# Rotating the first keys and queries on VectorE, with finer filling, in a fused attention and RWKV kernel

## The chip, the cores and the metric

One core of one Trainium2 chip runs the whole program. The metric is the device time of one execution in microseconds (us), the median of several runs. The profile is that of one execution, and its times count from the first instruction.

## The reference, cut to what matters

The program is a first block of two layers and a second block of one layer on 512 tokens of width 1024, all in float32. The diff touches the first block:

```python
def first_block(x, p, ...):
    for i in range(2):
        h = rms_norm(x, norm_g[i])
        y = mixer_a(...) if i == 0 else mixer_b(h, b_w_in, b_q_norm, b_k_norm, b_w_out)
        x = x + y                                   # the mixer ends with @ w_out
        g = sigmoid(rms_norm(x, ple_norm_g[i]) @ ple_w_gate[i])
        x = x + g * (p[i] @ ple_w_proj[i])
    return rms_norm(x, final_norm_g)

def mixer_b(h, ...):                                # 16 query heads, 4 key heads of width 64
    q, k, v, gate = split(h @ w_in)
    q = rope(rms_norm(q, q_norm_g)); k = rope(rms_norm(k, k_norm_g))
    o = softmax(q k^T / 8) v                        # all 512 keys
    return (o * silu(gate)) @ w_out
```

`rope` multiplies each row by a table of cosines and adds the row with swapped quarters times a table of sines. The kernel folds the norm's gain (and 1/8 for the queries) into the tables.

## The kernel before

The program is written in Python over tiles. A planner puts each engine's instructions in an order by a model of their times, with the order of the program as the priority; each engine then runs its own list strictly in that order, and waits are by tile and buffer.

Matrix products keep float32 precision by splitting each operand into a high part (rounded) and a low part (the rest) and adding three products. So each weight unit (512 KB) is loaded by SP's DMA queue (`wraw`), copied to its high part by ScalarE (`whi`, line 147) and subtracted to its low part (`wlo`, line 148) by the engine that `self.lo` names: VectorE, or GpSimd once `mixer_b` has made its first queries.

`rows` makes token-major products (line 200), `cols` feature-major ones (lines 183 to 185). Results lie in PSUM banks by tag: two banks each of `mm`, `sc`, `tr` and `u`.

`mixer_b` first makes keys and values, then the queries of group 0 (four heads), then loops over four groups. `qk_rows` makes 256 tokens' worth of keys or queries in each of two passes: products into a bank; square on ScalarE into `b_scr` (line 529); sum, reciprocal root and multiply on VectorE into `b_qn` (lines 531 to 535); rotation on GpSimd, one multiply by the cosines into `b_rot` (line 540) and four by the sines into a second `b_scr` (line 546); an add on VectorE (line 550). `b_scr` and `b_qn` have one buffer each. Then follow two steps that transpose the result (line 555) and split it into `b_Q` (or `b_Kh` and `b_Kl`); the second half of each step in `group` makes a gate by `cols`.

In the loop a group has four sets of two blocks (`b_block`); a block makes the scores of 128 queries for two heads (lines 638 and 639), their negated maximum `b_mn` on VectorE (641), the exponential into `b_P` on ScalarE (644; six buffers), the reciprocal `b_rd` (646), the scaling on GpSimd (647), transposes (654), a split into `b_ph` and `b_pl` (216 and 217) and the products with V (661). After each set, `next(fill)` runs one of the four steps of the next group's `group` generator, so that TensorE has other work; in the last group the steps are parts of the output projection over the first six of eight feature blocks (`first`), at most six of eight parts.

After the mixer the rest of `first` is run; then `load_p` loads p on SP's queue (line 391) and splits it into `p_hi` and `p_lo`. In layer 0, `rope_tables` also loads the tables (lines 505 to 510), and `products` multiplies them by the gains on VectorE (line 515, 16 instructions). Then come the last part of the output projection, with its add to x on VectorE (line 342), the norm, and the gate with p's projection (`ple`).

Of the kernel before, what the change touches and what calls it, by code (L numbers as in the profile page):

```python
# [10 lines left out]
F32 = mybir.dt.float32  # L11
# [8 lines left out]
KT = 8  # L20
TT = 4
# [102 lines left out]
class Net:  # L124
# [50 lines left out]
    def cols(self, key, act):  # L175

        nc = self.nc
        self.fetch(key)
        wh, wl = self.w.pop(key)
        ah, al = act  # L180
        ps = self.bank("mm")
        for kt in range(KT):
            nc.tensor.matmul(ps, lhsT=wh[:, kt], rhs=ah[:, kt], start=kt == 0, stop=False)  # L183
            nc.tensor.matmul(ps, lhsT=wh[:, kt], rhs=al[:, kt], start=False, stop=False)  # L184
            nc.tensor.matmul(ps, lhsT=wl[:, kt], rhs=ah[:, kt], start=False, stop=kt == KT - 1)  # L185
        return ps
# [201 lines left out]
    def load_p(self, l, pool):  # L388
        nc = self.nc
        raw = pool.tile([P, 2, S], F32, name="p_raw", bufs=1)  # L390
        nc.sync.dma_start(out=raw, in_=self.a["pT"][l])
        hi = pool.tile([P, 2, S], F32R, name="p_hi", bufs=1)
        lo = pool.tile([P, 2, S], F32R, name="p_lo", bufs=1)
        self.split(hi, lo, raw)
        return hi, lo
# [102 lines left out]
    def rope_tables(self, keep, pool, name, scale):  # L498
# [13 lines left out]
        def products():  # L512
            for j, o in enumerate((c, s)):
                for tt in range(TT):
                    nc.vector.scalar_tensor_tensor(o[:, tt], t[:, j, tt], scale, g[:, j], op0=OP.mult, op1=OP.mult)
# [3 lines left out]
    def qk_rows(self, pool, us, act, tabs, evac, bank="mm"):  # L519

        nc = self.nc
        c, s = tabs
        rot = pool.tile([P, TT, 256], F32, name="b_rot", bufs=1)
        for tp in range(2):
# [3 lines left out]
            sq = pool.tile([P, 512], F32, name="b_scr", bufs=1)  # L528
# [5 lines left out]
            qn = pool.tile([P, 512], F32, name="b_qn", bufs=1)  # L534
# [5 lines left out]
            nc.gpsimd.tensor_tensor(r4, q4, c[:, ts, None, :].to_broadcast([P, 2, 4, HD]), op=OP.mult)  # L540
            t2 = pool.tile([P, 512], F32, name="b_scr", bufs=1)
            for tt in range(2):
                for hf in range(2):
                    vw = lambda ap: ap.rearrange("p (h s f e) -> p h s f e", h=4, s=2, f=2)
                    sv = s[:, 2 * tp + tt].rearrange("p (s f e) -> p s f e", s=2, f=2)[:, :, hf]
                    nc.gpsimd.tensor_tensor(vw(t2[:, 256 * tt:256 * tt + 256])[:, :, :, hf],
# [4 lines left out]
            yield  # L551
        for pr in range(2):
            ps = self.bank("tr")
            for t in range(TT):
                nc.tensor.transpose(ps[:, t * P:(t + 1) * P], rot[:, t, pr * P:(pr + 1) * P], self.ident)
            evac(pr, ps)
            yield

    def mixer_b(self, act, oT, pool, last):
# [17 lines left out]
        for tp, _ in enumerate(self.qk_rows(pool, us, act, tk, put_k, "u")):  # L577
# [7 lines left out]
        def group(g, Q, gates):  # L585

            gp = g % 2
            self.fetch(("b_q", g, 0), ("b_q", g, 1))
# [9 lines left out]
            for n, _ in enumerate(self.qk_rows(pool, us, act, tq, put_q, "sc" if g == 0 else "mm")):  # L598
                if n > 1:
                    ps = self.cols(("b_g", 2 * g + n - 2), act)  # L600
# [9 lines left out]
        self.lo = nc.gpsimd  # L610
        for g in range(4):
            Qn, gn = [], []
            fill = group(g + 1, Qn, gn) if g < 3 else last
            for pr in range(2):
                i = 2 * g + pr
                for bp in range(2):
                    U = self.bank("u").rearrange("p (b e q) -> p b e q", b=2, e=2)
                    for bb in range(2):
                        self.b_block(pool, Q[2 * pr:2 * pr + 2], Kh[:, g], Kl[g // 2][:, g % 2], V[:, :, g], 2 * bp + bb, U[:, bb])
# [8 lines left out]
                    for _ in range(1 if g < 3 else 2 - bp):  # L628
                        next(fill, None)
# [774 lines left out]
def tile_net(ctx: ExitStack, tc: tile.TileContext, a, out, stop=None):  # L1404
# [22 lines left out]
    with ExitStack() as blk:  # L1427
# [25 lines left out]
        for l in range(2):  # L1453
            oT = N.new_act()
            with open_pool("pm%d" % l) as pool:
                first = N.out_proj(l, oT, (0, 1, 2))
                if l == 0:
                    N.mixer_a(act, oT, pool)
                else:
                    N.mixer_b(act, oT, pool, (next(first, None) for _ in range(6)))  # L1460
                for _ in first:
                    pass
# [3 lines left out]
            with open_pool("pn%d" % l) as pool:  # L1466
                act = N.new_act()
                pT = N.load_p(l, pool)
                g = N.gain(pool, "ple_norm_g", l)
                if l == 0:  # L1470
# [246 lines left out]
```

## Time and profile before

| | |
|---|---|
| median of 3 runs | 1243.92 us (1239.63 to 1244.29) |
| the profiled execution | 1243.45 us, span 1241.4 us |
| mean granted TensorE clock | 0.960 of 2.4 GHz |
| TensorE busy | 1145.3 us (92%) |
| VectorE, ScalarE, GpSimd busy | 849.4 us (68%), 624.0 us (50%), 425.6 us (34%) |

The span is from the first to the last instruction. Layer 0's last part of the output projection runs from about 287 us, the second mixer from about 380 to 647 us. A busy share is a mean over stages with different limits, so the rows that matter are those of single stretches.

### The profile page before, as it was taken

How to read it: one execution, taken by the hardware profiler on the slowest of the kernel's cores; microseconds unless marked ns; L12 is line 12 of the kernel's file. 1: busy time of each engine (PE TensorE's matmuls, PEld its weight loads, DVE VectorE, ACT ScalarE, POOL GpSimd, SP SyncE). 2: the span in 40 equal slices, each digit the busy share in tenths (PEclk: the TensorE clock that was granted, in tenths of full speed). 3: DMA queues.
4: the chain of work that ended last, by engine and by line, in shares of the span. 5: the costliest groups of instructions: out<-in, count | busy, mean ns of one | idle time of the engine just before them, and what ended most of it. 6: DMA issues, size and time to landing. Idle time of an engine off the chain costs nothing.

```text
span 1241.4 us, 20546 instructions
## 1 busy us (share of the span) xinstructions
PE 1145.3 (92%) x7176; PEld 1006.2 (81%) x7176; DVE 849.4 (68%) x2089; ACT 624.0 (50%) x1355; POOL 425.6 (34%) x571
## 2 busy tenths in 40 slices
PE   7999999997999879999999989798899789899995
PEld 6898989885889767888877889688898678798884
DVE  6566666655677678887766663488786924688846
ACT  5565565533552438676655642433544223267842
POOL 0021211110112555857320011163444623357851
PEclk9999999998999979999999999889789989899998
DMA  6333333213133210102132345684667543712511
GB/s 244 115 107 99 107 94 103 88 52 123 51 123 98 68 51 18 40 30 68 52 112 84 104 142 190 209 269 146 197 186 183 172 136 102 235 48 71 194 35 68
DMA packets 87041, 143.25 MB, mean 115 GB/s; under 512 B 21525, under 2 KB 52245, under 8 KB 86938
## 3 DMA queue, kind: packets, MB, share of 16 engines
q1 hardware_dynamic: 72632, 134.53, 34.5%
q10 hardware_dynamic: 13730, 5.31, 1.7%
q0 software_dynamic: 576, 2.10, 0.5%
q8 instruction: 56, 0.92, 0.3%
q14 instruction: 47, 0.39, 0.1%
HBM read 114.12 MB, written 27.79 MB: 114 GB/s over the span
## 4 chain that ended last, share of the span: by engine, by line
PE 64%; DVE 18%; DMA 8%; ACT 4%; issue 3%; POOL 1%; SPq 1%; ACTq 0%; DVEq 0%; POOLq 0%
PE mm L200 23%; PE mm L183 5%; PE mm L184 5%; PE mm L185 5%; PE mm L211 3%; PE u L661 2%; PE sc L200 2%; PE tr L654 2%; DVE KT L951 2%; PE tr L487 1%; PE ch L987 1%; DVE big L953 1%; PE u L1357 1%; PE tr L313 1%; DVE wlo L148 1%
## 5 line engine op out<-in xcount | busy, mean ns | idle before, releaser
L200 PE MATMUL mm<-whi,act 128*128 128x256 f32 (+2 forms) x1344 | 359.7, 325 | 16.5 <-DVE x L342 7.6
L200 PE MATMUL mm<-wlo,act 128*128 128x256 f32 (+2 forms) x896 | 288.6, 322 | 0.0
L200 PEld LDWEIGHTS mm<-whi,act 128*128 128x128 f32 x1344 | 241.7, 195 | 38.5 <-DVE x L342 10.5
L200 PEld LDWEIGHTS mm<-wlo,act 128*128 128x128 f32 x896 | 175.4, 196 | 10.1 <-issue 0.2
L147 ACT CAST whi<-wraw 128x1024 fp32r<-128x1024 f32 (+1 forms) x128 | 133.2, 1043 | 94.4 <-PE mm L200 36.1
L200 PE MATMUL mm<-whi,half 128*128 128x256 f32 (+1 forms) x448 | 146.0, 328 | 3.0 <-DVE half L217 3.0
L148 DVE TENSOR_TENSOR wlo<-wraw,whi 128x1024 fp32r<-128x1024 f32 x83 | 107.3, 1297 | 48.7 <-ACT whi L147 47.0
L148 POOL TENSOR_TENSOR wlo<-wraw,whi 128x1024 fp32r<-128x1024 f32 (+2 forms) x45 | 106.9, 2377 | 75.7 <-ACT whi L147 58.4
L183 PE MATMUL mm<-act,whi 128*128 128x512 f32 x312 | 125.8, 403 | 2.6 <-DVE b_qn L535 2.6
L185 PE MATMUL mm<-act,wlo 128*128 128x512 f32 x312 | 124.5, 399 | 0.0
L200 PEld LDWEIGHTS mm<-whi,half 128*128 128x128 f32 x448 | 88.4, 198 | 9.8 <-DVE half L217 4.0
L479 POOL TENSOR_SCALAR a_P<-a_P,a_rd 128x256 f32<-128x256 f32 x64 | 33.0, 519 | 156.5 <-DVE a_rd L478 143.8
L184 PE MATMUL mm<-half,whi 128*128 128x512 f32 x200 | 79.1, 396 | 0.0
L183 PEld LDWEIGHTS mm<-act,whi 128*128 128x128 f32 x312 | 60.1, 192 | 14.5 <-issue 3.5
L185 PEld LDWEIGHTS mm<-act,wlo 128*128 128x128 f32 x312 | 59.8, 192 | 11.8
L647 POOL TENSOR_SCALAR b_P<-b_P,b_rd 128x512 f32<-128x512 f32 x64 | 45.9, 724 | 44.5 <-DVE b_rd L646 32.9
L644 ACT ACTIVATE b_P<-sc,b_mn 128x512 f32<-128x512 f32 x64 | 44.1, 690 | 23.7 <-DVE b_mn L641 21.2
L217 DVE TENSOR_TENSOR b_pl<-tr,b_ph 128x512 fp32r<-128x512 f32 x64 | 43.7, 683 | 16.0 <-ACT b_ph L216 15.7
L473 DVE CUSTOM_DVE_ANT_0 a_P<-sc,a_bias 128x256 f32<-128x256 f32 x64 | 26.1, 422 | 34.7 <-PE tr L487 20.1
L641 DVE TENSOR_REDUCE b_mn<-sc 128x1 f32<-128x512 f32 x64 | 43.6, 684 | 8.1 <-PE sc L639 7.4
L385 POOL TENSOR_TENSOR x<-pu,x 128x512 f32<-128x512 f32 x8 | 10.3, 1293 | 111.6 <-DVE pu L383 111.6
L1343 POOL TENSOR_SCALAR n_P<-n_P,b_rd,n_gl 128x128 f32<-128x128 f32 (+3 forms) x64 | 39.3, 624 | 25.6 <-DVE b_rd L1341 6.2
(385 smaller groups left out, 2899.2 us busy)
## 6 DMA issues: line engine op xcount, KB each, us to landing
wraw<-in_wstream SPq DMA_DIRECT2D x133, 512.0 KB, 3.7
a_bias<-in_bias SPq DMA_DIRECT2D x16, 384.0 KB, 3.1
rkv<-d_raw SPq DMA_DIRECT2D x16, 384.0 KB, 4.9
d_raw<-act SPq DMA_DIRECT2D x8, 384.0 KB, 6.0
xf<-x SPq DMA_DIRECT2D x4, 512.0 KB, 3.7
d_low<-low ACTq DMA_DIRECT2D x8, 256.0 KB, 2.3
d_t<-rkv SPq DMA_DIRECT2D x8, 256.0 KB, 4.2
low<-d_low SPq DMA_DIRECT2D x8, 256.0 KB, 3.6
```

Of the source, the lines that this page charges most:

```text
L147: nc.scalar.copy(hi[:, :m], raw[:, :m])
L148: self.lo.tensor_tensor(lo[:, :m], raw[:, :m], hi[:, :m].bitcast(F32), op=OP.subtract)
L183: nc.tensor.matmul(ps, lhsT=wh[:, kt], rhs=ah[:, kt], start=kt == 0, stop=False)
L184: nc.tensor.matmul(ps, lhsT=wh[:, kt], rhs=al[:, kt], start=False, stop=False)
L185: nc.tensor.matmul(ps, lhsT=wl[:, kt], rhs=ah[:, kt], start=False, stop=kt == KT - 1)
L200: nc.tensor.matmul(ps, lhsT=l, rhs=r, start=i == 0, stop=i == len(ops) - 1)
L211: nc.tensor.matmul(ps, lhsT=l, rhs=r, start=i == 0, stop=i == len(ops) - 1)
L217: (eng_lo or nc.vector.tensor_sub)(lo, src, hi.bitcast(F32))
L641: nc.vector.tensor_reduce(mn, ps, axis=AX.X, op=OP.max, negate=True)
L644: nc.scalar.activation(pt, ps, AF.Exp, bias=mn, scale=1.0, accum_out=den)
L647: nc.gpsimd.tensor_scalar(pt, pt, rd, 0.5, op0=OP.mult, op1=OP.mult)
L1343: nc.gpsimd.tensor_scalar(w, w, rd, st["gl"][:, b, gc:gc + 1], op0=OP.mult, op1=OP.mult)
```

## The change

- `cols` becomes a generator `cols_parts` that can stop half-way.
- `load_p` issues its DMA on ScalarE's queue, and it runs before the rest of `first`, which is now drained behind it. For layer 1 five parts of `first` run in the loop and three are left.
- The tables' products run on GpSimd: two multiplies of 128x256 per table pair, and two scalings for the queries.
- Keys and the queries of group 0 (`early`) take their scratch from `b_P`, and their rotation runs on VectorE. Later groups stay on one buffer each and on GpSimd.
- The low parts of group 1's four weight units are made on VectorE (before: GpSimd).
- A group's `fill` has eight steps; one runs ahead of every block but the first, and what is left runs after the last.

```diff
     def cols(self, key, act):
+        return next(self.cols_parts(key, act, 1))
+
+    def cols_parts(self, key, act, parts):
...
         for kt in range(KT):
+            if kt and kt % (KT // parts) == 0:
+                yield None
             nc.tensor.matmul(ps, lhsT=wh[:, kt], rhs=ah[:, kt], start=kt == 0, stop=False)
...
-        return ps
+        yield ps
...
     def load_p(self, l, pool):
-        nc.sync.dma_start(out=raw, in_=self.a["pT"][l])
+        nc.scalar.dma_start(out=raw, in_=self.a["pT"][l])
...
         def products():
             for j, o in enumerate((c, s)):
-                for tt in range(TT):
-                    nc.vector.scalar_tensor_tensor(o[:, tt], t[:, j, tt], scale, g[:, j], op0=OP.mult, op1=OP.mult)
+                nc.gpsimd.tensor_tensor(o, t[:, j], g[:, j, None, :].to_broadcast([P, TT, HD]), op=OP.mult)
+                if scale != 1.0:
+                    nc.gpsimd.tensor_scalar(o, o, scale, None, op0=OP.mult)
...
     def qk_rows(self, pool, us, act, tabs, evac, bank="mm"):
+        early = bank != "mm"
+        scr = lambda name: pool.tile([P, 512], F32, name="b_P", bufs=6) if early else pool.tile([P, 512], F32, name=name, bufs=1)
+        E = nc.vector if early else nc.gpsimd
...
             for j in range(2):
                 self.rows(ps[:, 256 * j:256 * j + 256], us, act, 2 * tp + j)
-            sq = pool.tile([P, 512], F32, name="b_scr", bufs=1)
+                if j == 0 and not early:
+                    yield None
+            sq = scr("b_scr")
...
-            qn = pool.tile([P, 512], F32, name="b_qn", bufs=1)
+            qn = scr("b_qn")
...
-            nc.gpsimd.tensor_tensor(r4, q4, c[:, ts, None, :].to_broadcast([P, 2, 4, HD]), op=OP.mult)
-            t2 = pool.tile([P, 512], F32, name="b_scr", bufs=1)
+            E.tensor_tensor(r4, q4, c[:, ts, None, :].to_broadcast([P, 2, 4, HD]), op=OP.mult)
+            t2 = scr("b_scr")
...
-                    nc.gpsimd.tensor_tensor(vw(t2[:, 256 * tt:256 * tt + 256])[:, :, :, hf],
+                    E.tensor_tensor(vw(t2[:, 256 * tt:256 * tt + 256])[:, :, :, hf],
...
         def group(g, Q, gates):
+            self.lo = nc.vector if g < 2 else nc.gpsimd
...
-            for n, _ in enumerate(self.qk_rows(pool, us, act, tq, put_q, "sc" if g == 0 else "mm")):
-                if n > 1:
-                    ps = self.cols(("b_g", 2 * g + n - 2), act)
+            for n in self.qk_rows(pool, us, act, tq, put_q, "sc" if g == 0 else "mm"):
+                if n is not None and n > 1:
+                    for ps in self.cols_parts(("b_g", 2 * g + n - 2), act, 1 if g == 0 else 2):
+                        if ps is None:
+                            yield
...
-        self.lo = nc.gpsimd
         for g in range(4):
...
                     for bb in range(2):
+                        if (pr, bp, bb) != (0, 0, 0):
+                            next(fill, None)
                         self.b_block(...)
...
-                    for _ in range(1 if g < 3 else 2 - bp):
-                        next(fill, None)
+            for _ in fill if g < 3 else ():
+                pass
...
-                    N.mixer_b(act, oT, pool, (next(first, None) for _ in range(6)))
-                for _ in first:
-                    pass
+                    N.mixer_b(act, oT, pool, (next(first, None) for _ in range(5)))
...
                 pT = N.load_p(l, pool)
                 g = N.gain(pool, "ple_norm_g", l)
+                for _ in first:
+                    pass
```

## Rows read from the trace of the kernel before

**Rows 1.** The page: engines' busy time, and two of the costliest groups (line 148).

```profile
PE 1145.3 (92%) x7176; PEld 1006.2 (81%) x7176; DVE 849.4 (68%) x2089; ACT 624.0 (50%) x1355; POOL 425.6 (34%) x571
...
L148 DVE TENSOR_TENSOR wlo<-wraw,whi 128x1024 fp32r<-128x1024 f32 x83 | 107.3, 1297 | 48.7 <-ACT whi L147 47.0
L148 POOL TENSOR_TENSOR wlo<-wraw,whi 128x1024 fp32r<-128x1024 f32 (+2 forms) x45 | 106.9, 2377 | 75.7 <-ACT whi L147 58.4
```

**Rows 2.** Stretches: length, busy us (instructions) by engine, granted clock, DMA, GB/s.

```profile
290.00:300.00 10.00, 7.72 (x30) 5.66 (x29) 3.42 (x12) 2.69 (x7) 0.00 (x0) 0.95 0.32 115
300.00:310.00 10.00, 7.24 (x20) 5.34 (x21) 5.89 (x28) 2.90 (x7) 0.00 (x0) 0.73 0.23 83
410.00:420.00 10.00, 6.51 (x29) 5.05 (x27) 7.69 (x14) 5.95 (x10) 7.52 (x7) 1.00 0.24 75
420.00:430.00 10.00, 8.72 (x62) 8.72 (x63) 7.47 (x18) 2.03 (x3) 4.50 (x5) 0.83 0.36 105
430.00:440.00 10.00, 7.31 (x49) 6.43 (x48) 7.84 (x18) 4.31 (x7) 4.69 (x6) 0.89 0.15 46
440.00:450.00 10.00, 9.09 (x31) 6.80 (x30) 6.86 (x8) 4.29 (x9) 6.45 (x7) 0.77 0.19 60
450.00:460.00 10.00, 6.80 (x24) 5.33 (x25) 8.68 (x25) 4.19 (x10) 7.24 (x11) 0.66 0.18 52
460.00:470.00 10.00, 9.70 (x61) 8.36 (x59) 5.22 (x11) 5.26 (x11) 4.23 (x5) 1.00 0.00 0
490.00:500.00 10.00, 7.61 (x50) 6.00 (x48) 9.12 (x27) 7.98 (x18) 4.15 (x6) 1.00 0.01 2
540.00:550.00 10.00, 7.38 (x46) 5.59 (x45) 9.35 (x28) 8.08 (x20) 3.94 (x7) 1.00 0.00 1
640.00:650.00 10.00, 8.62 (x39) 6.49 (x38) 6.88 (x12) 5.43 (x14) 2.46 (x4) 1.00 0.51 192
650.00:660.00 10.00, 9.45 (x44) 7.52 (x44) 10.00 (x39) 7.30 (x15) 0.00 (x0) 1.00 0.59 179
```

The engines stand in the order TensorE products, TensorE weight loads, VectorE, ScalarE, GpSimd.

**Rows 3.** The chain that ended last, 280 to 440 us: start, length, what.

```profile
294.19 11.33 DMA rope_raw<-in_rope_b
```

**Rows 4.** Timeline, 278 to 322 us: start, length, engine, instruction, [idle before, releaser].

```profile
299.59 0.49 DVE L515 SCALAR_TENSOR_TENSOR b_k_norm_c<-rope_raw,rope_g 128x64 f32<-128x64 f32 x3 [4.28 <-DMA rope_raw<-in_rope_b]
...
305.54 0.63 DVE L515 SCALAR_TENSOR_TENSOR b_q_norm_c<-rope_raw,rope_g 128x64 f32<-128x64 f32 x4 [4.11 <-DMA rope_raw<-in_rope_b]
...
307.37 0.50 PE L200 MATMUL mm<-whi,act 128*128 128x512 f32 x1 [2.02 <-DVE x L342]
```

**Rows 5.** Timeline of ScalarE, 375 to 445 us.

```profile
431.76 0.60 ACT L529 ACTIVATE b_scr<-mm 128x512 f32<-128x512 f32 x1 [9.01 <-DVE b_rot L550]
```

**Rows 6.** Timeline of GpSimd, 375 to 445 us.

```profile
397.31 2.40 POOL L148 TENSOR_TENSOR wlo<-wraw,whi 128x1024 fp32r<-128x1024 f32 x1 [2.92 <-ACT whi L147]
...
416.08 1.69 POOL L546 TENSOR_TENSOR b_scr<-b_qn,b_q_norm_s 128x128 f32<-128x128 f32 x4
```

**Rows 7.** Timeline of VectorE, 375 to 445 us.

```profile
385.32 0.68 DVE L531 TENSOR_REDUCE b_ss<-b_scr 128x8 f32<-128x512 f32 x1
...
388.53 0.69 DVE L535 TENSOR_TENSOR b_qn<-u,rs_y 128x512 f32<-128x512 f32 x1
...
397.37 2.37 DVE L532 TENSOR_SCALAR b_ss<-b_ss 128x8 f32<-128x8 f32 x1
...
417.81 2.81 DVE L550 TENSOR_TENSOR b_rot<-b_rot,b_scr 128x512 f32<-128x512 f32 x1 [1.97 <-POOL b_scr L546]
```

**Rows 8.** Instructions that read b_Q: shortest, median, longest in ns; first and last start.

```profile
L638 PE MATMUL sc<-b_Kh,b_Q x64: 387/474/796, 435.3 to 629.6; 128*128 128x512 f32 x64
```

**Rows 9.** Instructions that write or read b_gate.

```profile
L626 POOL TENSOR_TENSOR b_sum<-b_sum,b_gate x16: 727/737/751, 471.7 to 645.2; 128x256 f32<-128x256 f32 x16
```

**Rows 10.** Groups by line and shape: busy us, mean ns.

```profile
L217 DVE TENSOR_TENSOR n_Vs<-mm,n_Vs 128x128 fp32r<-128x128 f32 x4 | 1.1, 283 | 0.0
```

**Rows 11.** Timeline of VectorE, 624 to 668 us.

```profile
651.37 1.21 DVE L217 TENSOR_TENSOR p_lo<-p_raw,p_hi 128x1024 fp32r<-128x1024 f32 x1
```

More of the change, by code (lines that the diff above doesn't have):

```diff
@@ L550, in qk_rows @@
             nc.vector.tensor_tensor(rv, rv, t2, op=OP.add)
-            yield
+            yield tp
         for pr in range(2):
@@ L556, in qk_rows @@
             evac(pr, ps)
-            yield
+            yield 2 + pr
     def mixer_b(self, act, oT, pool, last):
@@ L576, in mixer_b @@
         V = pool.tile([P, TT, 4, P], F32R, name="b_V", bufs=1)
-        for tp, _ in enumerate(self.qk_rows(pool, us, act, tk, put_k, "u")):
+        for tp in self.qk_rows(pool, us, act, tk, put_k, "u"):
             if tp > 1:
```

## Prediction

> **What bounds the kernel now.** I read the page first: TensorE is busy for 92% of the span [rows 1], so a change can win only where TensorE stands still or runs at its lower clock. The table by stretches of 10 us says where that is in the parts that the diff touches [rows 2]. From 410 to 470 us the idle time is 3.49 + 1.28 + 2.69 + 0.91 + 3.20 + 0.30 = 11.9 us; the granted clock falls to 0.83, 0.89, 0.77 and 0.66 after those gaps, and at that clock busy time is longer than its work by 0.17 x 8.72 + 0.11 x 7.31 + 0.23 x 9.09 + 0.34 x 6.80 = 6.7 us. So 18.6 us are lost there. From 290 to 310 us the same count gives 5.0 + 2.3 = 7.4 us. Two stretches inside the loop, at 490 and 540, lose 5.0 us, and the two after it, at 640 and 650, lose 1.9 us. These add up to 33 us, and nearly all that the change can give lies in them.
>
> Next I asked who is late in each. At 290 to 310, VectorE stands at the rotary table's first multiply until its DMA lands [rows 3, 4]: 4.28 us for the keys' table and 4.11 us for the queries'. Behind each of these stands an add of the output projection, which frees the accumulator that TensorE wants next; one of TensorE's two waits is shown, 2.02 us [rows 4].
>
> At 410 to 440 the first queries are late. A pass (square, sum, reciprocal root, normalise, rotate, add) uses one b_scr and one b_qn buffer, so the square of the next pass waits until the rotation of the last one is added: ScalarE stood 9.01 us for that [rows 5]. The rotation sits on GpSimd in a queue with the weights' low parts: a table multiply, four half-multiplies in 1.69 us, then a low part of 2.40 us [rows 6]. VectorE's own small instructions are held while GpSimd runs a low part: a 128x8 scaling that starts with one takes 2.37 us, and an add of 512 columns takes 2.81 us [rows 7]. The first scores start at 435.3 us [rows 8], while TensorE works off what doesn't depend on them and then waits.
>
> **The tables on GpSimd, and p.** VectorE no longer issues the 16 table multiplies and loses 4.28 + 4.11 = 8.4 us of standing. GpSimd issues four 128x256 multiplies and two scalings; it works at nothing else there (0.00 busy in both stretches [rows 2]), and the nearest multiply takes 0.74 us [rows 9], so some 4 us for all six. Its readers come some 90 us later [rows 4, 7]. What is late next is the chain of adds and norms on VectorE itself. While GpSimd multiplies, VectorE may be held, as it is beside the low parts [rows 7]: between 0 and 4 us. I take 1.4, since only a part of the multiplies will meet an instruction that matters, and so 7.0 us for this term (3 to 9).
>
> The Trainium skill speaks against this part: the GPSIMD Engine Reference (section Key points) says that GpSimd shares its SBUF interfaces with VectorE and contends with VectorE's two-port modes and with instructions of two SBUF inputs. The holds agree with it [rows 7]. If each of these multiplies held VectorE in full, the term would be 4.4 us and the sum 2.6 us less.
>
> p's load moves from SP's queue, where it stands behind three weight loads, to ScalarE's, and is issued before the last parts of the output projection. In the first layer that leaves SP one DMA fewer ahead of the gain; all transfers still land in the stretch in which the tables did. In the second layer p_lo takes 1.21 us of a VectorE that is full [rows 2, 11]. If it moves ahead of that stretch, 1.2 us are won. The three parts of the projection now left behind the load (two before) give TensorE something to do where it idles at 640. I take 1.5 us for the tail, from -2 (the load holds ScalarE for a while) to 3.
>
> **First keys and queries.** Scratch comes from six b_P buffers, three to a pass, so two passes overlap and the square no longer waits. The rotation runs on VectorE: per pass one multiply of 512 columns (0.69, as the normalising multiply [rows 7]) and four half-multiplies of 128 columns. Their bounds are 0.17 (a quarter of 0.69) and 0.28 us (a 128-column VectorE row of another stage [rows 10]); I take 0.28. That is 0.69 + 1.12 = 1.8 us of new VectorE work for each of four passes, 7.2 us. The group-1 low parts also move to VectorE: four units of 1.30 us [rows 1], 5.2 us, in place of 2.4 us each on GpSimd, and with them go the holds. Such holds cost VectorE 2.2 us in the scaling and 2.1 us in the add [rows 7]; four units carry about 8 us. So VectorE's total in this stretch hardly grows (7.2 + 5.2 - 8 = 4.4 us), and the standing goes.
>
> When would the first scores start? VectorE's first pass begins at 385.32 with the sum and ends its multiply at 389.2 [rows 7], 3.9 us with a value split of 512 columns (0.69) between; so 3.2 us and, with rotation and add, 3.2 + 1.8 + 0.7 = 5.7 us. Four passes are 22.8 us. By the code two value splits and four key splits (six at 0.69, 4.1 us) and up to eight low parts (group 0's four and group 1's four, 10.4 us) stand in the same queue. If VectorE never waits, it is through at 385.3 + 22.8 + 4.1 + 10.4 = 422.6. Transposes and the queries' split add about two 512-column instructions, 1.4 us, so the scores start near 424, 11 us earlier; if the four moved low parts fall behind the passes, near 419. Up to then TensorE has own work: it issues 29 + 62 + 49 products from 410 to 440 [rows 2], nearly all of them gates and the rows of the next group. So the idle time and the slow clock up to 440 (7.5 + 2.3 us) should go, nearly all. From 440 to 470 8.8 us are lost, partly as an aftermath, and partly because group 2's low parts still run on GpSimd and hold VectorE among the first blocks' maxima; I take 40% of it. Sum 9.5 + 3.5 = 13 us, bounds 4 (VectorE becomes the limit and the passes end where they do now, less the waits of the square) and 18.6 (all).
>
> **Filling in eight pieces.** The work is the same. The stretches at 490 and 540 show what lumps cost: VectorE is 91% and 93% busy there and TensorE waits for it, 5.0 us in both [rows 2]. A half-sized piece between every two blocks spreads the next group's pass over the loop. Against it: the engines' orders come from a planner, and a new order can open gaps in the dense stretches as well. I take 2.0 us, from -4 to 5.
>
> Sum: 7.0 + 13 + 2.0 + 1.5 = 23.5 us. The profiled execution took 1243.45 us, 0.5 below the median of the runs; 1243.5 - 23.5 = 1220, and I add 1 us because the terms share VectorE: **1221 us**.
>
> **Rivals.** (a) VectorE takes over as the limit. It is 77% busy from 410 to 440 [rows 2] and gets 12.4 us of new work. If the holds by GpSimd don't go away (group 2's low parts come forward into the places of group 1's), the middle term falls to 4 and the loop's to 0: 7 + 4 + 1.5 = 12.5, 1231 us. For it: VectorE's queue is strict, and any low part that is put ahead of a pass delays it by 1.3 us.
>
> (b) Nearly everything is recovered, since an earlier start also keeps the clock at its upper level (1.00 from 460 on [rows 2]) and the halves fill both loop gaps: 7.4 + 18 + 5 + 2 = 32, 1211 us.
>
> (c) Nothing moves: the planner puts the first scores where they were, behind the group-1 rows, and p and tables win under 6 us. Against it stands the 9.01 us wait [rows 5], whose cause is gone. 1240 us.
>
> (d) Slower: the fill. A block is a chain through four engines (scores, maximum, exponential, scaling, transposes, split), and TensorE hides it with the next group's work. With a piece ahead of every block, pieces and blocks alternate more finely, and a piece whose pass is late on VectorE stops TensorE in front of a block that could run. There are 7 such points in each of three groups and 5 in the last, 26; at 1.3 us each (half of a gap like that at 490 or 540 [rows 2]) the loop loses 34 us and the time is 1243.5 - 21.5 + 34 = 1256. From 0.8 us a point it takes all of the rest, from 1.1 the change is slower by over 0.5%. Against it: the longest gaps now follow lumps, not points.
>
> **How the numbers follow.** Chances: forecast (13 to 30 us won) 0.48; (a) 0.19; (b) 0.14; (c) 0.09; (d) 0.10. Some 0.5%, 6.2 us, is what a measurement of this kernel can tell from no change. Forecast, (a) and (b) are faster by more, 0.81; (c) is the same, 0.09; (d) slower, 0.10. The range takes in forecast, (a) and (b) without their far ends: 1205 to 1238. The likeliest case alone is 1213 to 1230.
>
> **What would show it.** Right: no VectorE wait on rope_raw near 300 and GpSimd multiplies in its place; squares of the first four passes that don't wait for b_rot; the first score matmul some 11 us closer to the keys' rows; a clock of 1.00 through what was 420 to 460; the 490 and 540 gaps smaller. Wrong: VectorE over 95% busy in the stretch after the keys, add or scaling instructions still at 2 us beside GpSimd low parts, ScalarE standing at the p_raw issue, or new TensorE gaps in the loop that end on b_pl or b_mn.

## The result and the profile after

| | before | after |
|---|---|---|
| median, same chip | 1243.72 us (1239.63 to 1244.29) | 1233.02 us (1231.49 to 1236.42) |
| ratio | | 0.9925, 95% interval 0.9895 to 0.9954 |
| profiled execution: span, mean clock | 1241.4 us, 0.960 | 1229.7 us, 0.969 |

The change won 10.7 us where 22.5 were forecast: the sign and the range held, the size did not. The page's engine line of after stands beside [rows 1]; GpSimd has 23.8 us less to do. VectorE's total hardly moves: the 16 table multiplies went, the rotations of four passes and four low parts came, and the standing beside GpSimd shrank.

```profile
PE 1141.6 (93%) x7176; PEld 1001.5 (81%) x7176; DVE 847.8 (69%) x2097; ACT 623.7 (51%) x1355; POOL 401.8 (33%) x553
...
L148 DVE TENSOR_TENSOR wlo<-wraw,whi 128x1024 fp32r<-128x1024 f32 x87 | 109.7, 1263 | 52.0 <-ACT whi L147 50.0
L148 POOL TENSOR_TENSOR wlo<-wraw,whi 128x1024 fp32r<-128x1024 f32 (+2 forms) x41 | 99.6, 2434 | 132.0 <-DVE rs_y L237 69.9
```

Landmarks cut both spans into stretches: the keys' first sum (the first b_ss), the first and the last b_sum of the loop, the last add of the layer's gate (pu), the end.

| stretch | before | after | difference | forecast |
|---|---|---|---|---|
| start to the keys' first sum | 385.3 | 375.4 | -9.9 | tables -7.0 |
| to the first b_sum | 84.0 | 72.7 | -11.3 | first keys and queries -13 |
| to the last b_sum | 175.4 | 182.6 | **+7.2** | eight pieces -2.0 |
| to the last pu | 71.6 | 72.1 | +0.5 | p and the tail -1.5 |
| to the end (no edit there) | 525.1 | 526.9 | +1.8 | 0 |

The sum is -11.7, the difference of the spans. The first two stretches together won 21.2 us where 20 were forecast. The loop lost where the forecast had it gain, and that is most of the miss.

**The tables.** The stretches of 10 us of after, columns as in [rows 2]; 290 to 310 is the same work as there, and 400 to 460 answers to 410 to 470 there, some 10 us earlier (400 to 410 is full, at clock 1.00):

```profile
290.00:300.00 10.00, 9.89 (x44) 7.98 (x45) 8.46 (x26) 5.37 (x13) 1.14 (x2) 1.00 0.29 100
300.00:310.00 10.00, 10.00 (x54) 8.35 (x53) 9.89 (x22) 7.91 (x15) 3.95 (x5) 1.00 0.48 165
...
410.00:420.00 10.00, 10.00 (x81) 9.79 (x80) 8.34 (x29) 3.47 (x6) 2.23 (x5) 1.00 0.18 54
420.00:430.00 10.00, 8.02 (x32) 5.23 (x30) 9.56 (x16) 5.22 (x10) 8.94 (x6) 1.00 0.33 105
430.00:440.00 10.00, 7.37 (x29) 5.98 (x30) 5.08 (x14) 1.92 (x5) 6.21 (x10) 0.83 0.17 52
440.00:450.00 10.00, 9.64 (x61) 8.17 (x60) 8.43 (x19) 9.10 (x22) 5.76 (x6) 1.00 0.18 52
450.00:460.00 10.00, 8.59 (x53) 6.53 (x52) 8.74 (x20) 9.02 (x22) 6.99 (x10) 1.00 0.01 3
```

TensorE is full from 290 to 310, but for 0.1 us, at clock 1.00, where it stood for 5 us and ran at 0.95 and 0.73 [rows 2]. From 310 to 320 it is full too (10.00, 1.00), where the kernel before still lost 1.0 us (0.26 of standing and 0.08 x 9.74):

```profile
310.00:320.00 10.00, 9.74 (x46) 7.79 (x45) 9.73 (x29) 7.04 (x13) 0.00 (x0) 0.92 0.38 114
```

The wait for the table's DMA has moved to GpSimd, which has nothing else to do (its timeline, with the last of the two scalings):

```profile
298.86 0.74 POOL L519 TENSOR_TENSOR b_k_norm_c<-rope_raw,rope_g 128x256 f32<-128x256 f32 x1 [30.56 <-DMA rope_raw<-in_rope_b]
...
304.80 0.74 POOL L519 TENSOR_TENSOR b_q_norm_c<-rope_raw,rope_g 128x256 f32<-128x256 f32 x1 [4.51 <-DMA rope_raw<-in_rope_b]
...
307.04 1.43 POOL L521 TENSOR_SCALAR b_q_norm_s<-b_q_norm_s 128x256 f32<-128x256 f32 x1
```

VectorE's timeline beside these multiplies:

```profile
298.19 0.22 DVE L243 SCALAR_TENSOR_TENSOR rs_t<-rs_y,rs_h 128x1 f32<-128x1 f32 x1
...
298.84 0.77 DVE L243 SCALAR_TENSOR_TENSOR rs_t<-rs_y,rs_h 128x1 f32<-128x1 f32 x1
299.54 0.68 DVE L347 TENSOR_TENSOR x<-mm,x 128x512 f32<-128x512 f32 x1
...
305.51 0.74 DVE L243 SCALAR_TENSOR_TENSOR rs_t<-rs_y,rs_h 128x1 f32<-128x1 f32 x1
306.28 0.33 DVE L248 SCALAR_TENSOR_TENSOR rs_t<-rs_t 128x1 f32<-128x1 f32 x1
306.54 1.21 DVE L148 TENSOR_TENSOR wlo<-wraw,whi 128x1024 fp32r<-128x1024 f32 x1
307.68 0.35 DVE L249 SCALAR_TENSOR_TENSOR rs_y<-rs_t,rs_y 128x1 f32<-128x1 f32 x1
```

The tiny instruction takes 0.22 us alone and 0.77 and 0.74 beside a multiply: two holds of some 0.5 us. Two more, beside the scalings, take 0.33 and 0.35 us (0.16 and 0.15 elsewhere in this stretch), so the holds come to 1.4 us in all. The adds from the accumulator, which set TensorE's pace here, take their 0.68 us. The Trainium skill's GPSIMD Engine Reference (section Key points), weighed ahead of the run, names VectorE instructions in a two-port mode or with two SBUF inputs as the ones that contend. The instruction held for 0.5 us has two, and the add has one operand from the accumulator, so these rows agree. The low part at 306.54 has two as well and kept its 1.21 us; beside it GpSimd's scaling took 1.43 us, where the one before took 0.85. The holds cost TensorE nothing that shows: it lost 0.1 us in these 20.

**The first passes.** ScalarE's squares no longer wait for a rotation, as they did in [rows 5]; its timeline:

```profile
374.70 0.60 ACT L541 ACTIVATE b_P<-u 128x512 f32<-128x512 f32 x1
381.04 0.59 ACT L541 ACTIVATE b_P<-u 128x512 f32<-128x512 f32 x1
389.76 0.60 ACT L541 ACTIVATE b_P<-sc 128x512 f32<-128x512 f32 x1 [3.22 <-PE sc L205]
402.00 0.60 ACT L541 ACTIVATE b_P<-sc 128x512 f32<-128x512 f32 x1
```

The four half-multiplies take 0.89 us on VectorE, 0.22 each; the forecast took 0.28.

**The loop.** TensorE's waits between the first and the last b_sum, after (us in total, times, longest):

```profile
PE u L677 <- DVE b_pl L222: 4.8, 9, 1.3
PE sc L654 <- ACT b_P L660: 1.8, 3, 0.8
PE u L677 <- ACT b_ph L221: 1.3, 4, 0.5
PE mm L205 <- DVE b_gate L618: 1.1, 2, 0.8
PE sc L654 <- DVE b_Q L608: 1.0, 2, 0.7
PE tr L670 <- DVE b_Q L608: 0.7, 2, 0.4
```

The waits of four whole steps (the first experiment) in the same stretch:

```profile
PE u L673 <- DVE b_pl L222: 4.8, 8, 1.2
PE sc L650 <- ACT b_P L656: 1.9, 3, 0.8
```

The old waits stay, and four come on top: for a split (b_ph), the next group's gate and its queries. These are waits of the pieces themselves and of blocks behind them: 1.3 + 1.1 + 1.0 + 0.7 = 4.1 us.

The gaps that the halves were to fill did not close. TensorE stood 5.0 us in the stretches at 490 and 540 [rows 2], at the first two group changes; in after the stretches just ahead of these changes are

```profile
472.00:482.00 10.00, 7.95 (x51) 6.56 (x52) 9.59 (x30) 7.28 (x17) 4.20 (x6) 1.00 0.01 2
520.00:530.00 10.00, 7.19 (x46) 5.50 (x45) 9.47 (x26) 5.89 (x14) 4.75 (x7) 1.00 0.00 1
```

which is 2.05 + 2.81 = 4.9 us, with VectorE 96% and 95% busy: the gaps only came forward by 8 us or so.

### The profile page after: what moved, and what is told of

The parts are those of the page before. It is cut to its first block, busy times and chain, and to the rows that moved or that the text cites. A ratio compares the mean times of both kernels' runs of the same rounds, so it can differ in the third digit from the quotient of the medians.

```text
span 1229.7 us, 20522 instructions
## 1 busy us (share of the span) xinstructions
PE 1141.6 (93%) x7176; PEld 1001.5 (81%) x7176; DVE 847.8 (69%) x2097; ACT 623.7 (51%) x1355; POOL 401.8 (33%) x553
## 4 chain that ended last, share of the span: by engine, by line
PE 61%; DVE 18%; DMA 6%; ACT 6%; issue 5%; POOL 3%; SPq 2%; ACTq 0%; DVEq 0%; POOLq 0%
PE mm L205 24%; PE mm L188 5%; PE mm L189 5%; PE mm L190 5%; PE sc L205 3%; PE mm L216 2%; PE u L677 1%; PE tr L492 1%; DVE KT L967 1%; PE tr L670 1%; DVE big L969 1%; PE ch L1003 1%; PE tr L318 1%; DMA rkv<-d_raw 1%; PE u L205 1%
## 5 line engine op out<-in xcount | busy, mean ns | idle before, releaser
L205 PEld LDWEIGHTS mm<-wlo,act 128*128 128x128 f32 x896 | 174.9, 195 | 10.3 <-POOL wlo L148 0.6
L148 POOL TENSOR_TENSOR wlo<-wraw,whi 128x1024 fp32r<-128x1024 f32 (+2 forms) x41 | 99.6, 2434 | 132.0 <-DVE rs_y L237 69.9
L188 PE MATMUL mm<-act,whi 128*128 128x512 f32 x312 | 125.4, 402 | 2.7 <-DVE b_qn L547 2.7
L660 ACT ACTIVATE b_P<-sc,b_mn 128x512 f32<-128x512 f32 x64 | 44.1, 690 | 21.5 <-DVE b_mn L657 13.5
L189 PE MATMUL mm<-act,whi 128*128 128x512 f32 x112 | 45.3, 404 | 0.0
```

The costliest lines, as they stand in the source:

```text
L148: self.lo.tensor_tensor(lo[:, :m], raw[:, :m], hi[:, :m].bitcast(F32), op=OP.subtract)
L205: nc.tensor.matmul(ps, lhsT=l, rhs=r, start=i == 0, stop=i == len(ops) - 1)
L660: nc.scalar.activation(pt, ps, AF.Exp, bias=mn, scale=1.0, accum_out=den)
```

## The experiments

Times in us. "Start" is from the keys' first sum to the first b_sum, "loop" from there to the last b_sum, "both" their sum, "late" from the last pu to the end, which no edit touches. The ratio is to the kernel before on the same chip (its medians were 1243.7 to 1245.2).

| run | median | ratio, 95% interval | start | loop | both | late |
|---|---|---|---|---|---|---|
| before | 1243.72 | 1 | 84.0 | 175.4 | 259.4 | 525.1 |
| after | 1233.02 | 0.9925 [0.9895, 0.9954] | 72.7 | 182.6 | 255.3 | 526.9 |
| e1_four_steps | 1227.4 | 0.9866 [0.9812, 0.9919] | 73.7 | 175.2 | 248.9 | 524.6 |
| e2_fill_only | 1254.63 | 1.0078 [1.0052, 1.0104] | 82.0 | 183.1 | 265.1 | 525.8 |
| e3_tables_only | 1235.29 | 0.9937 [0.9909, 0.9964] | 82.2 | 175.6 | 257.8 | 525.1 |
| e4_early_only | 1241.66 | 0.9969 [0.9939, 0.9999] | 72.4 | 175.3 | 247.7 | 538.9 |
| e5_eight_old_end | 1234.99 | 0.9923 [0.9899, 0.9947] | 72.7 | 183.4 | 256.1 | 526.8 |
| e6_four_new_end | 1232.99 | 0.9901 [0.9882, 0.9921] | 72.5 | 175.6 | 248.1 | 534.2 |
| e7_four_mid | 1240.82 | 0.9966 [0.9937, 0.9995] | 73.4 | 185.3 | 258.7 | 531.9 |
| e8_four_no_p | 1230.67 | 0.9882 [0.9851, 0.9913] | 73.6 | 175.1 | 248.7 | 530.7 |
| e9_six_q | 1231.3 | 0.9904 [0.9875, 0.9932] | 72.6 | 183.6 | 256.2 | 522.6 |
| e10_four_late | 1227.27 | 0.9871 [0.9831, 0.991] | 72.6 | 178.4 | 251.0 | 532.0 |
| e11_four_lo_pool | 1228.04 | 0.9879 [0.984, 0.9919] | 71.1 | 180.7 | 251.8 | 526.5 |
| e12_four_rot_pool | 1220.6 | 0.9823 [0.978, 0.9867] | 66.3 | 179.2 | 245.5 | 524.7 |
| e13_eight_late | 1231.94 | 0.9906 [0.9876, 0.9937] | 73.7 | 177.3 | 251.0 | 530.0 |
| e14_one_scratch | 1235.88 | 0.9938 [0.9911, 0.9964] | 73.3 | 182.5 | 255.8 | 525.7 |
| e15_scratch_only | 1233.8 | 0.9907 [0.9877, 0.9937] | 69.1 | 183.3 | 252.4 | 531.4 |
| e16_rot_pool_new_end | 1229.18 | 0.9873 [0.9835, 0.9911] | 67.5 | 179.5 | 247.0 | 531.0 |

The last column spans 16 us under edits that don't touch that code, so small effects are read from the stretch where the edit lies. Where the code up to a landmark is the same, the stretches agree: the start takes 72.7, 72.7 and 72.6 us in after, e5 and e9. Each profile is of one execution, in e4 and e10 the slowest one.

**One part at a time.** First the theory that the eight steps lose what the rest wins, against the theory that the early start is only borrowed and is given back in the loop.

e1 takes the changed kernel and puts the old fill back:

```diff
-                        if (pr, bp, bb) != (0, 0, 0):
-                            next(fill, None)
                         self.b_block(...)
...
+                    for _ in range(1 if g < 3 else 2 - bp):
+                        next(fill, None)
```

> The changed kernel with its filling put back to four steps per group and six parts of the projection in the last; all else as changed. Between the first and the last b_sum the changed kernel takes 182.6 us, the one before 175.4. Theory 1, the eight steps cost this: the stretch falls to about 175 and the time to 1226 us. Theory 2, the stretch is longer because filling that was once done ahead of the first block is now done in the loop: no change, 1231 to 1235 us.

The next three take the kernel before and give it one part of the diff alone: e2 the eight steps (`cols_parts`, the loop's `next(fill)`), e3 `products` on GpSimd, e4 the lines with `early`, `scr`, `E` and `self.lo`.

> The kernel before with the eight filling steps alone (and five parts of the projection in the last group, three drained where two were). Theory 1: slower by about 7 us, 1251 us. Theory 2: 1240 to 1245 us.

> The kernel before with the table products on GpSimd alone. The keys' first sum came 9.9 us earlier in the changed kernel. If the tables alone did this: 1234 us, and the first sum near 375.5. If p's earlier load did a part: 1237 us, first sum near 378.

> The kernel before with the scratch in b_P, the rotation of keys and first queries on VectorE and group 1's low parts on VectorE, and nothing else. The changed kernel won 11.3 us between the keys' first sum and the first b_sum. Theory 1: the gain stays, 1232 us. Theory 2: it is borrowed from the filling and comes back in the loop, 1238 to 1240 us.

Measured: without the eight steps the loop is back at 175.2 (e1), and with them alone it is 183.1 and the kernel is slower than before (e2). The early start is not given back: e4 is 10.8 us ahead of before at the last pu. Its time doesn't show that: the late column grew by 13.8 in the profile, which is of the slowest of its ten executions (1246.15 us, the fastest 1236.79). The tables alone give 9.1 us at the keys' first sum (376.2 for 385.3), without p's move.

**Which of the steps cost.** e5 keeps eight steps in groups 0 to 2 and gives the last group its old six parts behind the sets; e6 is the reverse; e7 keeps four whole steps and calls each between the two blocks of a set; e8 undoes p's move on e1.

```diff
 e5:
+                        if g < 3 and (pr, bp, bb) != (0, 0, 0):
...
+                    for _ in range(0 if g < 3 else 2 - bp):
+                        next(fill, None)
...
 e6:
+                        if g == 3 and (pr, bp, bb) != (0, 0, 0):
...
+                    for _ in range(1 if g < 3 else 0):
+                        next(fill, None)
...
 e7:
                     for bb in range(2):
+                        if g < 3 and bb:
                             next(fill, None)
                         self.b_block(...)
...
+                    for _ in range(0 if g < 3 else 2 - bp):
+                        next(fill, None)
...
 e8:
-        nc.scalar.dma_start(out=raw, in_=self.a["pT"][l])
+        nc.sync.dma_start(out=raw, in_=self.a["pT"][l])
```

> Changed kernel, but the last group goes back to six parts of the output projection taken after the sets; groups 0 to 2 keep their eight steps. Theory 1 (the loss of 7.2 us has two parts that lie in their own places): the stretch from the last maximum to the last sum of the loop falls from 17.0 to 14.0 us, the stretch from the first sum to the last maximum stays near 165.5, and the time is 1230 us. Theory 2 (the loss at the end is only the echo of the late groups before it): the end stays at 17 us and the time near 1233. Theory 3 (eight steps in groups 0 to 2 cost nothing, all comes from the last group): first sum to last maximum 161.2, time 1227.

> Four whole steps after the sets in groups 0 to 2, but the changed kernel's last group: five parts of the output projection, one ahead of each block. Theory 1: last maximum to last sum 17.0 us, first sum to last maximum 161.2, time 1230 us. Theory 2: 14 us at the end and 1227.4. Theory 3: the whole loss, 1233.

> Four whole steps, each between the two blocks of a set in place of behind the set; the last group as before. If the number of points decides (half-sized pieces cut the next group's pass in two and keep its bank twice as long), first sum to last sum stays at 175 us and the time at 1227. If the place decides (a step between the two blocks of a set keeps the second block's scores from covering the first block's chain), first sum to last sum is 179 us or more and the time 1231 or more.

> Four steps, and p loaded as before (on SP's queue, behind the rest of the output projection): tables and start alone. If p's move is worth nothing, as the equal stretch of 24.3 us behind the mixer says: 1227.4 us, and from the mixer's end to the end of the program as in the four-step kernel. If the load ahead of the projection's parts is worth the forecast's 1.5 us, 1229. If the 13.8 us that the start alone lost in the second block come without p's move, 1238.

My first theory, that 3.0 of the 7.2 us lie in the last group, fell: with the old last group the loop stays at 183.4, and with the new last group alone it is 175.6. All of it comes from groups 0 to 2. And e7 loses more with four whole steps (185.3) than eight halves do, so the number of pieces is not the cause; their place is. p's move: up to the last pu, e8 is at 697.0 and e1 at 698.2. It gives nothing.

**Why the place.** Either the next group's work waits for buffers that the blocks still hold, or it stands ahead of blocks that could run. e9 is the changed kernel with six b_Q buffers (b_sum gives up one). e10 calls four whole steps between the two blocks again, but one block late in place of one block early (in sets 2, 3 and 4, the last step behind the group). e13 calls eight halves, the first one behind the second block:

```diff
 e9:
+                    q = pool.tile([P, S], F32R, name="b_Q", bufs=6)
...
 e10:
+                        if g < 3 and bb and (pr, bp) != (0, 0):
                             next(fill, None)
...
 e13:
+                        if g < 3 and (pr, bp, bb) > (0, 0, 1):
                             next(fill, None)
```

> Changed kernel with six b_Q buffers in place of five (b_sum gives up one of its two for the room). With eight steps the next group's fourth query tile is asked for ahead of the group's last block, which still reads the buffer that it would get; with six there is a free one. If the loop's loss comes from such buffers, first sum to last sum falls from 182.6 to 178 us or less and the time to 1228. If it comes from the place of the steps alone, it stays within 1 us of 182.6 and the time near 1233.

> Four whole steps again between the two blocks of a set, but half a set later in place of half a set earlier: in the second, third and fourth set, and the last step behind the group. If it is bad as such that a step parts the two blocks of a set, first sum to last sum is 182 us or more and the time 1235 or more, as with the steps half a set early (185.3). If only the early call is bad (the next group's work is put ahead of blocks that could run, and its buffers are not free yet), it is 175 to 178 us and the time 1227 to 1230.

> Eight half-steps in groups 0 to 2, but the first one behind the second block in place of the first, so that no half comes earlier than in the four-step kernel and every second one comes a block later; last group as before. From the end of the first set to the end of the last the four-step kernel takes 173.1 us, the one with eight steps and the old last group 181.4. If the early call is what costs, 173 to 176 us here and a time near 1228. If the number of pieces costs, wherever they stand, 180 us or more and 1234.

The b_Q buffers are not the cause: the loop stays at 183.6 with six, and TensorE's waits for the queries stay too (1.0 + 0.8 us in e9). Other buffers, such as the two banks of `mm` that a gate holds, were not tried. The same whole steps cost 10.1 us a block early and 3.2 a block late, the same halves 8.2 early (e5) and 2.1 late (by "both" against e1: 9.8 and 2.1, 7.2 and 2.1). TensorE's waits in e13's loop:

```profile
PE u L679 <- DVE b_pl L222: 6.3, 11, 1.3
PE sc L656 <- ACT b_P L662: 1.9, 4, 0.8
PE mm L205 <- DVE x L347: 0.2, 1, 0.2
```

The waits for the gate and the queries are gone; the blocks' own b_pl waits grew from 4.8 to 6.3. So most of the loss is the early call. Some 2 to 3 us remain in both late runs; whether they come from parting the blocks or from the later call, these runs don't tell. Between first and last b_sum, TensorE's idle time is 7.6 us in e1 and 11.9 in after; that is 4.3 of the 7.4. The rest is busy time, 170.7 for 167.6 us with nearly the same products (1046 and 1047 recorded), whose single durations add up to 340.1 us in both: by the records, whose ends are modelled, they overlap less. What keeps them from overlapping the records don't show; that stays open.

**Which part of the start.** e11 and e12 are e1 with group 1's low parts, and with the rotation, back on GpSimd; e14 is e1 with one b_scr and one b_qn; e15 has only the six-buffer scratch (both others back); e16 is e12 with the new last group.

```diff
 e11, e15:
+            self.lo = nc.vector if g < 1 else nc.gpsimd
...
 e12, e15, e16:
+        E = nc.gpsimd
...
 e14:
+        scr = lambda name: pool.tile([P, 512], F32, name=name, bufs=1)
```

> Four-step kernel with group 1's four low parts back on GpSimd; scratch and rotation as changed. From the keys' first sum to the loop's first sum the four-step kernel takes 73.7 us, the kernel before 84.0. The holds that the prediction priced at 8 us of VectorE against 5.2 us of its own work would make this 3 to 5 us longer: 77 to 79 us and a time of 1231. If VectorE's own low parts cost as much as the holds, 73 to 74 us and no change.

> Four-step kernel with the rotation of the keys and the first queries back on GpSimd; six-buffer scratch and low parts as changed. If the wait of the square for the scratch was what made the start late, the gain stays: 73 to 76 us from the keys' first sum to the loop's first sum, time near 1228. If the rotation's place in GpSimd's queue was, most is lost: 80 us or more and a time of 1234 or more.

> Four-step kernel with one b_scr and one b_qn buffer for all groups; rotation and low parts on VectorE as changed. From the keys' first sum to the end of the first group's last set the kernel before takes 112.5 us, the four-step kernel 102.2. If the six-buffer scratch is the source of the start's gain, 108 us or more and a time of 1234. If the rotation on VectorE shortens the chain so far that the single buffer no longer holds the square, 101 to 104 us and 1227 to 1229.

> Four-step kernel with the scratch change alone: rotation and group 1's low parts are back on GpSimd. From the kernels with one of the two back (98.9 us with the rotation, 105.1 us with the low parts, 102.2 with neither) the two effects add to 101.8 us from the keys' first sum to the end of the first group's last set, and a time of 1223 to 1226. If GpSimd's queue gets too long with both (rotation behind low parts, as before), 107 us or more and a time of 1231.

> The best so far (four steps, rotation on GpSimd; 1220.6) with the changed kernel's last group (five parts of the output projection, one ahead of each block), which gave 13.2 us in place of 14.0 between the last maximum and the last sum. If that adds, 1219.8 by the profile's stretches, not to be told from 1220.6 by the times; the second block, which no edit touches, moves more than that from kernel to kernel.

An earlier first b_sum leaves more of the next group's work to the loop, so here the whole way is read ("both"; it holds 1479 to 1482 recorded products in every run). Against e1's 248.9, the low parts on GpSimd cost 2.9 (e11; the loss lies in the loop, the start is 71.1 where 77 to 79 was expected), and the rotation on GpSimd *wins* 3.4 (e12). Against before's 259.4, the rest with one buffer each wins 3.6 (e14), the scratch alone 7.0 (e15), both together 10.5 (e1): they add. Read only to the end of the first group's last set, as it was expected for e14 and e15, the wins are nearer to each other: before 112.5, e14 104.2, e15 103.1, e1 102.2, e11 105.1, e12 98.9, so 8.3, 9.4 and 10.3. (e13, e14 and e15 have another order behind it: group 3 takes 51.2 us with 276 products, for 47.0 with 256 in e1.) So the scratch alone gives most of the gain by either reading, and the rest without it by the shorter one only. They are not the same cure: the fourth square starts 36.1 us behind the first in before, still 33.3 in e14, 27.3 in e1, and 21.5 in e15 and e12. The best is the scratch with the low parts, and without the rotation: 13.9 over the whole way, 13.6 to the end of the first group. e16's new last group was not to be told apart, as expected (both 247.0 and 245.5); its median is 8.6 us above e12's, of which 6.3 are in the late column. Several totals missed what was expected by 4 to 10 us (e4, e6, e13, e14, e15).

VectorE's timeline in after, from the last rotation to the split of the queries:

```profile
413.60 0.69 DVE L562 TENSOR_TENSOR b_rot<-b_rot,b_P 128x512 f32<-128x512 f32 x1
414.21 0.68 DVE L543 TENSOR_REDUCE b_ss<-b_scr 128x8 f32<-128x512 f32 x1
...
417.74 0.68 DVE L608 TENSOR_TENSOR b_Q<-tr,b_Q 64x512 fp32r<-64x512 f32 x1
419.34 1.41 DVE L608 TENSOR_TENSOR b_Q<-tr,b_Q 64x512 fp32r<-64x512 f32 x2 [0.92 <-ACT b_Q L607]
```

In between, ScalarE's copy that this split reads, and TensorE's transposes and first scores:

```profile
416.55 0.58 ACT L607 CAST b_Q<-tr 64x512 fp32r<-64x512 f32 x1 [3.10 <-PE tr L567]
```

```profile
416.13 0.60 PE L567 MATMUL tr<-ident,b_rot 128*128 128x128 f32 x4
...
422.73 0.39 PE L654 MATMUL sc<-b_Kh,b_Q 128*128 128x512 f32 x1
```

The same in e12, VectorE and TensorE, and GpSimd's rotation there:

```profile
410.19 2.88 DVE L560 TENSOR_TENSOR b_rot<-b_rot,b_P 128x512 f32<-128x512 f32 x1 [1.20 <-POOL b_P L556]
414.21 0.68 DVE L606 TENSOR_TENSOR b_Q<-tr,b_Q 64x512 fp32r<-64x512 f32 x1 [1.15 <-ACT b_Q L605]
```

```profile
413.12 0.66 PE L565 MATMUL tr<-ident,b_rot 128*128 128x128 f32 x4 [0.45 <-DVE b_rot L560]
...
417.32 0.40 PE L650 MATMUL sc<-b_Kh,b_Q 128*128 128x512 f32 x1
```

```profile
380.86 3.69 POOL L556 TENSOR_TENSOR b_P<-b_P,b_k_norm_s 128x128 f32<-128x128 f32 x4
...
407.19 1.29 POOL L550 TENSOR_TENSOR b_rot<-b_P,b_q_norm_c 128x512 f32<-128x512 f32 x1 [6.71 <-DVE b_P L545]
408.44 1.71 POOL L556 TENSOR_TENSOR b_P<-b_P,b_q_norm_s 128x128 f32<-128x128 f32 x4
```

A rotation takes 1.29 + 1.71 us on GpSimd and 0.69 + 0.89 on VectorE; two of the four in e12, beside low parts on VectorE, take 3.69 and 3.54 us in place of the 1.71. The Trainium skill's GPSIMD Engine Reference (section Key points) calls VectorE about twice as fast in elementwise work, and the undisturbed rows agree. But VectorE is the busier engine: in after it is 87% busy from 380 to 420 (34.93 of 40 us).

In after the last rotation is added at 414.29, and the first scores start 8.4 us later. VectorE's order puts the next group's whole first pass (414.21 to 417.7) ahead of the split, but that holds the split by 0.6 us only, since the copy that it reads ends at 417.13. The rest stands in TensorE's own list: the transposes start 1.8 us after the add, behind products of the next group's rows, and the first scores 2.7 us after the second split ends (420.05), behind products of a gate. TensorE is full all that while. In e12 the rotation is done at 413.07 in spite of an add held for 2.88 us, the transposes follow at 413.12, the split at 414.21, and the first scores start at 417.3 in place of 422.7. So the rotation on GpSimd comes with an order in which transposes and scores stand earlier. Whether this order or the time freed on VectorE makes the 3.4 us was not tried.

## Why the prediction was right and wrong

**Right in mechanism.** The tables' wait moved to GpSimd and nothing reads them for long. The term was undersized (9.9 for 7.0, above its 3 to 9): of the 8.4 us that TensorE lost from 290 to 320 it now loses 0.1, so the 1.4 us of holds that VectorE does have cost nothing, and the 1.4 us taken off for them were too much. The size is not sharp: the keys' first sum lies at 375.4 to 377.6 us in the fifteen profiles with the tables on GpSimd, and at 385.3 to 386.2 in the three without. For the first passes the square's wait went, and the clock is 1.00 from 380 to 430. The loss from 400 to 460, counted as in the forecast, is 7.6 us in place of 18.6, 11.0 less, and the stretch shows 11.3 (13 forecast). What is left lies at 420 to 440, where low parts on GpSimd hold an add for 2.88 us once more, as rival (a) said. The first scores did not come as forecast: 47.3 us behind the keys' sum (422.7 less 375.4), 50.0 before, and 39 in the working. The chain of passes was worked out well (its last add ends 38.8 us behind that sum, for 37.3), but the scores then came 8.4 us later and not 1.4: the working counted the split and the transposes, and not TensorE's own list, in which rows and a gate of its other work stand ahead of them. The gain is there all the same, since TensorE is full with these products until the scores.

**The step that failed: "filling in eight pieces".** It was put at -2.0 and measured +7.2. The prediction read the gaps at 490 and 540 as the price of lumps and took finer pieces as their cure. Rival (d) had the mechanism, a piece in front of a block that could run, but wrongly as a price per point: the same number of points a block later costs 2.1 us, and the last group's five points cost nothing (e6). The bound of 4 us worse was too narrow. The gaps belong to the group changes: they have their size in e1, where the four steps stand as before (2.6 us at 474 to 486 and 2.7 at 522 to 534), and with the halves (4.9 us in both, 8 us earlier). So finer pieces did not fill them, and TensorE's idle time elsewhere in the loop grew from 2.4 to 7.0 us.

**Also mis-sized.** In "p and the tail" the stretch from the last b_sum to the last pu takes 72.1 us for 71.6. The load came later in its stage, and not earlier (issues of p's load, shortest, median and longest in ns, first and last start; before and after):

```profile
L391 SPq DMA_DIRECT2D p_raw<-in_pT x2: 333/358/383, 286.1 to 638.2; - x2
```

```profile
L396 ACTq DMA_DIRECT2D p_raw<-in_pT x2: 334/337/340, 286.2 to 632.0; - x2
```

SP issued it 6.5 us ahead of the last b_sum, ScalarE's queue 1.3 us behind it, and p_lo starts 8.6 us behind, where it was 6.7 [rows 11]. In e8, with the old queue, both are back (6.7 and 71.6 us).

The rotation's cost on VectorE was counted (6.3 us measured: four times 0.69 + 0.89; 7.2 forecast), but as a price worth paying; e12 shows that without it the way to the last b_sum is 3.4 us better. Together: +9.2 for the loop, +1.7 for the start, +2.0 to the last pu, +1.8 behind it, -2.9 for the tables and -1.0 for the term that was added for sharing make 10.8 us, and the miss from 1243.5 - 22.5 is 10.8 by the spans. That the time lies near rival (a)'s 1231 is luck: (a) has 4 for the first passes and 0 for the loop, and they measured 11.3 and -7.2.

## What to carry to other kernels

- Work that fills another stage's waits belongs behind the work whose waits it fills: the same halves cost 8 us a block early and 2 a block late. Before cutting pieces finer, ask which of them now stands ahead of something that could run.
- When one wait is removed in two ways at once (more buffers, and a faster engine for what they waited for), try each alone. Here more buffers and the low parts won 13.9 us of the way, and 10.5 with the rotation on the faster, but busier, engine as well; the version with the rotation on GpSimd and four steps takes 1220.6 us, 0.9823 of before (four executions, 1219.6 to 1229.0), and is the best of the study.
- Where a planner orders the program, an edit changes stages far away. Sizes under 1% are read from landmarks around the edit, and not from the total.

## What was not expected

The second block, which no edit touches, takes 522.6 to 538.9 us (the last column of the table). Its stage of masked maxima starts 158.0 to 158.6 us before the end in eight of the eighteen profiles (before and after among them) and 162.9 to 171.3 us in the other ten: the planner orders it in other ways, even where only the last group's parts of the projection differ (e12 and e16). The stretch from the last pu to the end in e1, e12, e16 and e4, columns as in [rows 2]:

```profile
698.20:1222.80 524.60, 466.35 (x3344) 419.50 (x3342) 358.92 (x963) 227.35 (x537) 223.13 (x259) 0.94 0.50 152
```

```profile
693.20:1217.90 524.70, 467.25 (x3344) 420.80 (x3342) 355.72 (x963) 227.81 (x537) 221.66 (x259) 0.94 0.50 152
```

```profile
696.60:1227.60 531.00, 471.67 (x3344) 424.24 (x3342) 356.70 (x963) 226.05 (x537) 226.51 (x259) 0.93 0.50 150
```

```profile
705.50:1244.40 538.90, 479.21 (x3343) 432.08 (x3342) 358.74 (x963) 226.29 (x537) 224.91 (x259) 0.92 0.49 148
```

The products are the same (3344, one record fewer in e4) and VectorE's work is equal to 1%; TensorE's busy time grows by 12.9 us from e1 to e4 and its granted clock falls from 0.94 to 0.92, while its idle time is 58.3 and 59.7 us. So most of the 14.3 us between e1 and e4 goes with the lower clock, and of e16's 6.3 us against e12 4.4 are busy time. The order is not all of it: e5 and e9 have the same order of instructions on every engine here and take 526.8 and 522.6 us, so some 4 us belong to the single execution. Which gap drops the clock was not tried.
